# A token mixer in a new order: one rescaling of the input, 18 slabs by seven products, gates and retention in DRAM

## The chip, the core and the metric

One core of a Trainium2 chip runs the whole program in one launch. The metric is the device time in microseconds (us) of one execution. The engines are named as the profile names them: PE is TensorE's matmul, PEld its load of the stationary operand, DVE is VectorE, ACT is ScalarE, POOL is GpSimd, SP is SyncE, whose queue issues nearly all DMAs here. Each engine takes its instructions in the order in which they stand in its queue, and waits on semaphores for the others.

## What is computed

One encoder block over 512 positions of width 1024, in float32. The two feed-forward blocks are SwiGLU with 2816 hidden columns; the change leaves them alone, apart from shared helpers.

```python
x = x + 0.5 * swiglu_ffn(rms_norm(x, ffn1_norm), ffn1_w_gate, ffn1_w_up, ffn1_w_down)
h = rms_norm(x, mix_norm)
u_a, v_a, q_r, k_r, v_r, g_r, gate_a, gate_b = split(h @ w_in + b_in)      # eight times 1024 columns
a = spatial_gating(gelu(u_a), gelu(v_a), ...)        # layer norm of v, a 128x128 matrix per group and chunk
q, k = rotary(q_r), rotary(k_r) / 16                 # four heads of 256
r = bidirectional_retention(q, k, v_r, decay)        # scores x decay^|distance|, then x v
r = r * rsqrt(mean(r * r) + eps) * silu(g_r)         # per head
mix = sigmoid(gate_a) * (a @ w_branch_a) + sigmoid(gate_b) * (r @ w_branch_b)
x = x + mix @ w_out
x = x + 0.5 * swiglu_ffn(rms_norm(x, ffn2_norm), ...)
return rms_norm(x, final_norm)
```

## The kernel before

Activations lie with their columns on the partitions, eight tiles of 128 x 512 for the width of 1024. Every float32 product is made of three matmuls: each operand is split into a high part `hi` (rounded to the matmul's type) and a rest `lo`, and `mm3` (L96 to L99) adds hi x hi, hi x lo and lo x hi. So each weight slab of 1024 x 256 (1 MB) is loaded into `raw` (pool `wp`, two buffers), cast to `whi` by ACT (L91) and subtracted to `wlo` by DVE (L93), in the pool `wh` with three buffers of each. Activations are split likewise (`split`, L81 and L83). PSUM has eight banks.

A plain slab takes 2 x 8 x 3 = 48 matmuls over 512 columns. The feed-forward blocks also have the seven-product scheme of Strassen and Winograd for many of their slabs: `fast_weights` makes three sums of quarters of the weights (`s1`, `s2`, `s4`) and `Fast` runs seven products of half size, 7 x 4 x 3 = 84 matmuls over 256 columns, in four steps, with copies and additions of the partial results on ACT and DVE; it reads the input in four combined forms (`tforms`), which are made once per block.

The mixer (L577 to L833) uses plain slabs only. Its input `h2` is x times the norm's weight, not yet divided by the root mean square; that factor, `bc`, is multiplied into each projection as it leaves PSUM. For each of four heads come `rot` (q and k, with rotation by `cos` and `sin`), `pv_mm` of the head before (`pr`, with its norm `nr`), for even heads the v block `tok_block`, `scores` (times the decay table `E`), and `gate_r` (g, Silu), which also calls `r_out`. Then come the two halves of the gating unit's v (`pva`), the slabs of u with the chunk matrices (`psg`), and the merge: for each of four column groups the gates ga and gb (`pgt`), `pa` (a times `wa`) and `pb` (r times `wb`). r, a and the gates stay on the chip. A scheduler places the instructions of all engines in a fixed order when the program is built, from the order of the code, the data and the free buffers.

Of the kernel before, what the change touches and what calls it, by code (L numbers as in the profile page):

```python
# [40 lines left out]
def block_kernel(ctx, tc, xT, wg1, wu1, wd1, w_in, wa, wb, wo, wg2, wu2, wd2, cols_d, rows_d, ws_d, cos_d, sin_d, out, out_t):  # L41
# [152 lines left out]

    def ffn(tag, x, h, norm, wg, wu, wd, on_x, col, fp, p_fast, first=None, last=None, last_weights=None, aside=None):
# [16 lines left out]

        def make_tforms():

            left = [fp_n]

            def F(name):
                if left[0] > 0:
                    left[0] -= 1
                    return fp.tile([P, S], F32R, tag="f", name=name)  # L220
                return A(name)

            H = S // 2
            for k in range(KT // 2):
                ys = []
                for kk in (k, k + KT // 2):
                    y = T(f"{tag}y")
                    nc.scalar.activation(y, x[kk], AF.Copy, scale=cols[:, col + kk:col + kk + 1])
                    ys.append(y)
                y11, y12, y21, y22 = ys[0][:, 0:H], ys[0][:, H:S], ys[1][:, 0:H], ys[1][:, H:S]  # L230
                ta, tb = T(f"{tag}ta"), T(f"{tag}tb")
                t1, t2, t3, t4 = ta[:, 0:H], ta[:, H:S], tb[:, 0:H], tb[:, H:S]
                nc.vector.tensor_tensor(out=t1, in0=y12, in1=y11, op=ALU.subtract)
                nc.vector.tensor_tensor(out=t2, in0=y22, in1=t1, op=ALU.subtract)
                nc.vector.tensor_tensor(out=t3, in0=y22, in1=y12, op=ALU.subtract)
                nc.vector.tensor_tensor(out=t4, in0=y21, in1=t2, op=ALU.subtract)
                for i, t in ((1, ta), (3, tb)):
                    hi, lo = F(f"{tag}t_hi"), F(f"{tag}t_lo")
                    nc.scalar.copy(hi, t)
                    nc.vector.tensor_tensor(out=lo, in0=t, in1=hi.bitcast(F32), op=ALU.subtract)  # L240
                    tforms[i, k] = hi[:, 0:H], lo[:, 0:H]
                    tforms[i + 1, k] = hi[:, H:S], lo[:, H:S]

        def fast_weights(w, p):

            name = f"{tag}f"
            K2 = KT // 2
            raw = wp.tile([P, KT, 2 * P], F32, tag="raw", name=name + "_raw")
            nc.sync.dma_start(out=raw, in_=w[:, p * 256:(p + 1) * 256].rearrange("(k p) c -> p k c", p=P))
            x11, x12, x21, x22 = (raw[:, a * K2:(a + 1) * K2, i * P:(i + 1) * P] for i in range(2) for a in range(2))  # L250

            def V(t):
                return t.rearrange("p (k c) -> p k c", c=P)

            s1, s2, s4 = T(name + "_s1"), T(name + "_s2"), T(name + "_s4")
            nc.vector.tensor_tensor(out=V(s1), in0=x21, in1=x22, op=ALU.add)  # L256
            nc.vector.tensor_tensor(out=x21, in0=x11, in1=x21, op=ALU.subtract)
            hi = wh.tile([P, KT, 2 * P], F32R, tag="whi", name=name + "_whi")
            nc.scalar.copy(hi, raw)  # L259
            nc.vector.tensor_tensor(out=V(s2), in0=V(s1), in1=x11, op=ALU.subtract)  # L260
            nc.vector.tensor_tensor(out=V(s4), in0=x12, in1=V(s2), op=ALU.subtract)
            p1 = split(s1, name + "_s")
            lo = wh.tile([P, KT, 2 * P], F32R, tag="wlo", name=name + "_wlo")
            nc.vector.tensor_tensor(out=lo, in0=raw, in1=hi.bitcast(F32), op=ALU.subtract)  # L264
            p2 = split(s2, name + "_s")
            p4 = split(s4, name + "_s")
            f = {}
            for nm, a, i in (("X11", 0, 0), ("X12", 1, 0), ("S3", 0, 1), ("X22", 1, 1)):
                f[nm] = [tuple(t[:, a * K2 + k, i * P:(i + 1) * P] for t in (hi, lo)) for k in range(K2)]
            for nm, part in (("S1", p1), ("S2", p2), ("S4", p4)):  # L270
                f[nm] = [tuple(t[:, k * P:(k + 1) * P] for t in part) for k in range(K2)]
            return f

        class Fast:

            def __init__(self, f, t):
                self.f, self.t = f, t
                H = S // 2  # L280
                self.a, self.v, self.b = (PS(f"{tag}pf")[:, 0:H] for _ in range(3))
                self.c11, self.c12, self.c21, self.c22 = t[0][:, 0:H], t[0][:, H:S], t[1][:, 0:H], t[1][:, H:S]

            def prod(self, o, xf, yf, first):
                for k in range(KT // 2):
                    mm3(o, *self.f[xf][k], *yf(k), first and k == 0, k == KT // 2 - 1, not first)

            def run(self, step):
                H = S // 2

                def Y(a, j):
                    return lambda k: tuple(t[:, j * H:(j + 1) * H] for t in h[a * (KT // 2) + k])

                def Tf(i):
                    return lambda k: tforms[i, k]

                if step == 0:
                    self.prod(self.a, "X11", Y(0, 0), True)
                    self.prod(self.v, "S1", Tf(1), True)
                    nc.scalar.copy(self.c11, self.a)  # L300
                    nc.scalar.copy(self.c22, self.v)
                elif step == 1:
                    self.prod(self.a, "S2", Tf(2), False)
                    self.prod(self.b, "X12", Y(1, 0), True)
                    nc.scalar.copy(self.c12, self.a)
                    nc.vector.tensor_tensor(out=self.c11, in0=self.b, in1=self.c11, op=ALU.add)
                elif step == 2:
                    self.prod(self.a, "S3", Tf(3), False)
                    self.prod(self.v, "S4", Y(1, 1), False)
                    nc.vector.tensor_tensor(out=self.c22, in0=self.a, in1=self.c22, op=ALU.add)  # L310
                    nc.vector.tensor_tensor(out=self.c12, in0=self.v, in1=self.c12, op=ALU.add)
                else:
                    self.prod(self.a, "X22", Tf(4), False)

            def scaled(self):

                H = S // 2
                nc.vector.tensor_tensor(out=self.t[0], in0=self.t[0], in1=bc, op=ALU.mult)
                yield self.t[0]
                nc.vector.tensor_tensor(out=self.c21, in0=self.a, in1=bc[:, 0:H], op=ALU.mult)  # L320
                nc.vector.tensor_tensor(out=self.c22, in0=self.c22, in1=bc[:, H:S], op=ALU.mult)
                yield self.t[1]
# [724 lines left out]
```

## Time and profile before

| | us |
|---|---|
| three runs, median (lowest to highest) | 1251.41 (1251.28 to 1252.13) |
| the profiled execution, its own time | 1251.25 |
| its span, first to last instruction | 1249.2 |
| PE busy | 1240.2 |
| DVE busy | 827.1 |
| ACT busy | 500.7 |

Between the span and the time of the profiled execution lie 2.05 us. A matmul's busy time overlaps the next one's, so what a matmul costs is read from the distance of starts. A row of a timeline has the start, the duration, engine, line and operation, output and inputs by the program's names, and in brackets how long the engine was idle ahead of it and what ended that.

### The profile page before, as it was taken

The numbers are of one execution on the slowest core, as the hardware profiler recorded it, in microseconds if no ns is written. First come the engines' busy times: TensorE is split into PE (matmuls) and PEld (weight loads), VectorE is DVE, ScalarE is ACT, GpSimd is POOL, SyncE is SP. The second block draws the span as 40 slices with busy tenths as digits, with TensorE's granted clock in tenths as the row PEclk, the third lists the DMA queues.
The fourth block names the chain that finished last, engine by engine and source line by source line (L and its number), as shares of the span: only waits on it lengthen the run. The fifth ranks groups of instructions, "written<-read, shape, count | busy, mean of one in ns | idle before, by whom it ended". The sixth has DMA issues, their size and how long they took to land.

```text
span 1249.2 us, 15979 instructions
## 1 busy us (share of the span) xinstructions
PE 1240.2 (99%) x6714; PEld 1076.0 (86%) x6714; DVE 827.1 (66%) x1148; ACT 500.7 (40%) x643; POOL 7.6 (1%) x12
## 2 busy tenths in 40 slices
PE   9999999999999999999999999999999999999997
PEld 7889899989878888888888888888888989998997
DVE  6796679657777575675298334445587665976674
ACT  6553245424443342434344222223364423542352
POOL 0000000000000000000000000000000000000000
PEclk9999999999999999999999999999999999999999
DMA  8234323430463222233223333324232242334121
GB/s 264 75 101 136 101 68 102 135 102 26 127 222 99 75 69 93 68 101 135 68 68 101 101 101 102 101 93 149 96 98 92 82 135 68 102 102 135 60 93 68
DMA packets 115944, 128.47 MB, mean 103 GB/s; under 512 B 2977, under 2 KB 105377, under 8 KB 115873
## 3 DMA queue, kind: packets, MB, share of 16 engines
q1 hardware_dynamic: 115296, 126.63, 31.7%
q8 instruction: 52, 0.85, 0.3%
q10 hardware_dynamic: 576, 0.84, 0.2%
q14 instruction: 20, 0.16, 0.0%
HBM read 123.26 MB, written 4.19 MB: 102 GB/s over the span
## 4 chain that ended last, share of the span: by engine, by line
PE 92%; issue 6%; DVE 0%; POOL 0%; DMA 0%; ACT 0%; POOLq 0%; ACTq 0%
PE bpf L97 4%; PE bpf L99 4%; PE bpf L98 4%; PE apf L97 3%; PE apf L99 3%; PE apf L98 3%; PE bpd L97 3%; PE bpd L99 3%; PE bpd L98 3%; PE apd L97 2%; PE apd L98 2%; PE pgt L98 2%; PE pgt L97 2%; PE pgt L99 2%; PE apd L99 2%
## 5 line engine op out<-in xcount | busy, mean ns | idle before, releaser
L97 PE MATMUL apd<-ahid_hi,ad_whi 128*128 128x512 f32 x176 | 68.5, 389 | 0.0
L98 PE MATMUL apd<-ahid_lo,ad_whi 128*128 128x512 f32 x176 | 68.5, 389 | 0.0
L99 PE MATMUL apd<-ahid_hi,ad_wlo 128*128 128x512 f32 x176 | 68.5, 389 | 0.0
L97 PE MATMUL bpd<-bhid_hi,bd_whi 128*128 128x512 f32 x128 | 49.8, 389 | 0.0
L98 PE MATMUL bpd<-bhid_lo,bd_whi 128*128 128x512 f32 x128 | 49.8, 389 | 0.0
L99 PE MATMUL bpd<-bhid_hi,bd_wlo 128*128 128x512 f32 x128 | 49.8, 389 | 0.0
L81 ACT CAST bf_s_hi<-bf_s 128x512 fp32r<-128x512 f32 x42 | 25.7, 622 | 37.9 <-DVE bf_s L256 16.9
L81 ACT CAST af_s_hi<-af_s 128x512 fp32r<-128x512 f32 x42 | 25.8, 621 | 37.5 <-DVE af_s L256 16.1
L803 DVE TENSOR_TENSOR gt<-pgt,n_bc 128x512 f32<-128x512 f32 x16 | 11.1, 691 | 43.2 <-PE pgt L99 43.2
L99 PEld LDWEIGHTS apd<-ahid_hi,ad_wlo 128*128 128x128 f32 x176 | 33.0, 188 | 6.9
L97 PEld LDWEIGHTS apd<-ahid_hi,ad_whi 128*128 128x128 f32 x176 | 33.1, 188 | 6.8
L98 PEld LDWEIGHTS apd<-ahid_lo,ad_whi 128*128 128x128 f32 x176 | 33.1, 188 | 6.6
L259 ACT CAST af_whi<-af_raw 128x2048 fp32r<-128x2048 f32 x14 | 26.8, 1914 | 23.0 <-PE apd L98 17.5
L83 DVE TENSOR_TENSOR af_s_lo<-af_s,af_s_hi 128x512 fp32r<-128x512 f32 x42 | 28.7, 685 | 10.6 <-ACT af_s_hi L81 8.2
L83 DVE TENSOR_TENSOR bf_s_lo<-bf_s,bf_s_hi 128x512 fp32r<-128x512 f32 x42 | 28.6, 684 | 10.6 <-ACT bf_s_hi L81 8.2
L259 ACT CAST bf_whi<-bf_raw 128x2048 fp32r<-128x2048 f32 x14 | 26.8, 1913 | 21.5 <-PE bpd L98 17.3
L264 DVE TENSOR_TENSOR bf_wlo<-bf_raw,bf_whi 128x2048 fp32r<-128x2048 f32 x14 | 32.0, 2287 | 4.7 <-ACT bf_whi L259 4.6
L264 DVE TENSOR_TENSOR af_wlo<-af_raw,af_whi 128x2048 fp32r<-128x2048 f32 x14 | 32.0, 2287 | 3.5 <-ACT af_whi L259 3.5
L408 DVE SCALAR_TENSOR_TENSOR x<-apd,x 128x512 f32<-128x512 f32 x24 | 16.2, 685 | 24.1 <-PE apd L99 24.1
L99 PE MATMUL apf<-h_hi,af_wlo 128*128 128x256 f32 x112 | 31.7, 283 | 0.0
L97 PE MATMUL bpf<-bt_hi,bf_s_hi 128*128 128x256 f32 x112 | 31.7, 283 | 0.0
L99 PE MATMUL bpf<-h_hi,bf_wlo 128*128 128x256 f32 x112 | 31.7, 283 | 0.0
(470 smaller groups left out, 4176.8 us busy)
## 6 DMA issues: line engine op xcount, KB each, us to landing
af_raw<-in_wg SPq DMA_DIRECT2D x8, 1024.0 KB, 5.3
ad_raw<-in_wd SPq DMA_DIRECT2D x8, 1024.0 KB, 5.2
bf_raw<-in_wg SPq DMA_DIRECT2D x8, 1024.0 KB, 5.3
bd_raw<-in_wd SPq DMA_DIRECT2D x8, 1024.0 KB, 5.2
af_raw<-in_wu SPq DMA_DIRECT2D x6, 1024.0 KB, 5.3
bf_raw<-in_wu SPq DMA_DIRECT2D x6, 1024.0 KB, 5.4
bu_raw<-in_wu SPq DMA_DIRECT2D x5, 1024.0 KB, 5.4
au_raw<-in_wu SPq DMA_DIRECT2D x4, 1024.0 KB, 5.8
```

The lines of the kernel that those rows point to most:

```text
L81: nc.scalar.copy(hi, src)
L83: nc.vector.tensor_tensor(out=lo, in0=src, in1=hi.bitcast(F32), op=ALU.subtract)
L97: nc.tensor.matmul(o, lhi, rhi, start=first, stop=False, skip_group_check=more)
L98: nc.tensor.matmul(o, lhi, rlo, start=False, stop=False, skip_group_check=more)
L99: nc.tensor.matmul(o, llo, rhi, start=False, stop=last, skip_group_check=more)
L259: nc.scalar.copy(hi, raw)
L264: nc.vector.tensor_tensor(out=lo, in0=raw, in1=hi.bitcast(F32), op=ALU.subtract)
L408: nc.vector.scalar_tensor_tensor(out=x[m], in0=pd[j], scalar=0.5, in1=x[m], op0=ALU.mult, op1=ALU.add)
L803: nc.vector.tensor_tensor(out=t, in0=pg, in1=bc, op=ALU.mult)
```

## The change

The seven-product helpers (`t_forms`, `fast_weights`, `Fast`, `Plain`) are moved out of `ffn`, with the weights, the name and the inputs as arguments; their arithmetic is the same. In the mixer, 18 of the slabs of 256 columns now run by seven products: q and k of heads 2 and 3, g and ga of heads 1 to 3, all of u and gb. After the first q, k and v block, `rescale` multiplies x by the norm's weight and `bc` once, and all later projections read it (`hs`, and `tforms` made from it), so that their factor `bc` is dropped. Two slabs run as a pair, step by step in turn (`pair`): q with k, g with ga, u with gb. Gates ga and gb are thus made early; they and the retention's output r are written to DRAM (`g_dram`, `r_dram`) and read back in the merge, which runs all of `pb` first and then all of `pa`. The decay table `E` is made per head (`decay`) rather than for all four ahead.

```diff
@@ helpers, now outside of ffn @@
+    def t_forms(name, get, pool, left):
...
+    def fast_weights(w, c0, name):
+        raw = wp.tile([P, KT, 2 * P], F32, tag="raw", name=name + "_raw")
+        nc.sync.dma_start(out=raw, in_=w[:, c0:c0 + 256].rearrange("(k p) c -> p k c", p=P))
...
+        s1, s2, s4 = T(name + "_s1"), T(name + "_s2"), T(name + "_s4")
+        nc.vector.tensor_tensor(out=V(s1), in0=x21, in1=x22, op=ALU.add)
+        nc.vector.tensor_tensor(out=x21, in0=x11, in1=x21, op=ALU.subtract)
+        hi = wh.tile([P, KT, 2 * P], F32R, tag="whi", name=name + "_whi")
+        nc.scalar.copy(hi, raw)
+        nc.vector.tensor_tensor(out=V(s2), in0=V(s1), in1=x11, op=ALU.subtract)
+        nc.vector.tensor_tensor(out=V(s4), in0=x12, in1=V(s2), op=ALU.subtract)
+        p1 = split(s1, name + "_s")
+        lo = wh.tile([P, KT, 2 * P], F32R, tag="wlo", name=name + "_wlo")
+        nc.vector.tensor_tensor(out=lo, in0=raw, in1=hi.bitcast(F32), op=ALU.subtract)
+        p2 = split(s2, name + "_s")
+        p4 = split(s4, name + "_s")
...
+        def through(self, func, b1, b2):
+            nc.scalar.activation(self.t[0], self.t[0], func, bias=b1)
+            nc.scalar.activation(self.c21, self.a, func, bias=b2)
+            nc.scalar.activation(self.c22, self.c22, func, bias=b2)
+            return self.t
@@ the mixer @@
+    def pair(name, one, two, mid=None):
+        slabs = [Fast(w, name, hs, tforms) if isinstance(w, dict) else Plain(w, name, hs) for w in (one, two)]
+        for step in range(4):
+            for sl in slabs:
+                sl.run(step)
+            if step == 1 and mid is not None:
+                mid()
+        return slabs
+    def gate_out(slab, i, mp):
+        off = (OFF_GA, OFF_GB)[i] + 256 * mp
+        for j, t in enumerate(slab.through(AF.Sigmoid, bias(off), bias(off + P))):
+            nc.sync.dma_start(out=g_dram[i][256 * mp + P * j:256 * mp + P * (j + 1), :], in_=t)
+    def scores(hd, q, k):
+        E = decay(hd)
...
+    def r_out(hd, rt, slab):
+        col = OFF_G + 256 * hd
+        for d, g in enumerate(slab.through(AF.Silu, bias(col), bias(col + P))):
+            nc.vector.tensor_tensor(out=rt[d], in0=rt[d], in1=g, op=ALU.mult)
+            nc.sync.dma_start(out=r_dram[256 * hd + P * d:256 * hd + P * (d + 1), :], in_=rt[d])
+    def rescale():
+        for k in range(KT):
+            nc.vector.scalar_tensor_tensor(out=x[k], in0=x[k], scalar=cols[:, C_GM + k:C_GM + k + 1], in1=bc,
+                                           op0=ALU.mult, op1=ALU.mult)
+            hs.append(split(x[k], "hs"))
+    def g_pair(hd, st, wg_, wf, i, mp):
+        rt = []
+        slabs = pair("pg", wg_, wf, lambda: rt.extend(r_norm(st)))
+        return lambda: (r_out(hd, rt, slabs[0]), gate_out(slabs[1], i, mp))
...
+        for hd in range(1, HEADS):
+            qk = pair("qk", wq, wk)
+            if hd == 1:
+                tforms.update(t_forms("mt", lambda i: x[i], tp, tp_n))
+                del x
+            get = plain_w if hd == 1 else fast_w
+            wg_ = get(OFF_G + 256 * (hd - 1), "g")
+            q = rot(qk[0].plain(), OFF_Q, hd, "q")
+            st = pv_mm(hd - 1, v, pt)
+            k = rot(qk[1].plain(), OFF_K, hd, "k")
+            wf = get(OFF_GA + 256 * (hd - 1), "ga")
+            if hd == 2:
+                b_row = bvr_t(1)
+                pv = tok_block(hs, OFF_VR + 512, "pv")
...
+            end = g_pair(hd - 1, st, wg_, wf, 0, hd - 1)
+            if hd < HEADS - 1:
+                wq, wk = fast_w(OFF_Q + 256 * (hd + 1), "q"), fast_w(OFF_K + 256 * (hd + 1), "k")
+            end()
+            pt = scores(hd, q, k)
...
+    w1 = fast_w(OFF_G + 256 * 3, "g")
+    v_half(0, lambda: last_st.append(pv_mm(HEADS - 1, v, pt)))
+    w2 = fast_w(OFF_GA + 256 * 3, "ga")
+    end = g_pair(3, last_st.pop(), w1, w2, 0, 3)
+    w1 = fast_w(OFF_U, "u")
+    end()
+    v_half(1)
+    v_stats()
+    w2 = fast_w(OFF_GB, "gb")
+    for p in range(4):
+        slabs = pair("pu", w1, w2)
+        if p < 3:
+            w1, w2 = fast_w(OFF_U + 256 * (p + 1), "u"), fast_w(OFF_GB + 256 * (p + 1), "gb")
+        else:
+            tb = load_w(wb, 0, KT, 0, 256, "wb")
+        u_out(slabs[0], p)
+        gate_out(slabs[1], 1, p)
+        if p == 0:
+            v_norm(0)
+        elif p < 3:
+            s_pair(p - 1)
+    for i in range(KT):
+        t = T("rl")
+        nc.sync.dma_start(out=t, in_=r_dram[P * i:P * (i + 1), :])
+        r.append(split(t, "r"))
+    for mp in range(4):
+        gates = gate_in(1, mp)
+        for j in range(2):
+            pb = PS("pb")
+            proj(pb, tb, j, r)
+            nc.vector.tensor_tensor(out=gates[j], in0=pb, in1=gates[j], op=ALU.mult)
...
-        gates = []
-        for off, wt in ((OFF_GA, tga), (OFF_GB, tgb)):
-            for j in range(2):
-                pg = PS("pgt")
-                proj(pg, wt, j, h2)
-                t = T("gt")
-                nc.vector.tensor_tensor(out=t, in0=pg, in1=bc, op=ALU.mult)
-                nc.scalar.activation(t, t, AF.Sigmoid, bias=bias(off + P * (2 * mp + j)))
-                gates.append(t)
```

Where the order of the engines changes, first on DVE, around the v block of head 2. Before, from the first of its two low halves (`pv_wlo`) to the second:

```order
L93 TENSOR_TENSOR pv_wlo<-pv_raw,pv_whi 128x2048
L83 TENSOR_TENSOR r_lo<-rt,r_hi 128x512 x2
L646 TENSOR_TENSOR g<-pg,n_bc 128x512 x2
L608 TENSOR_TENSOR qt<-q,n_bc 128x512 x2
L615 SCALAR_TENSOR_TENSOR qc<-qt,cols,cos 128x512
L617 SCALAR_TENSOR_TENSOR qs<-qt,cols,sin 128x512
L615 SCALAR_TENSOR_TENSOR qc<-qt,cols,sin 128x512
L618 TENSOR_TENSOR qc<-qc,qs 128x512
L617 SCALAR_TENSOR_TENSOR qs<-qt,cols,cos 128x512
L93 TENSOR_TENSOR pv_wlo<-pv_raw,pv_whi 128x2048
```

The second one stands among the q rotation of head 2, before anything that reads `pr` of head 1. Now, from the k rotation and the norm's split to the first `pv_wlo`:

```order
L654 TENSOR_TENSOR kc<-kc,ks 128x512
L653 SCALAR_TENSOR_TENSOR ks<-qk_t,cols,cos 128x512
L238 TENSOR_TENSOR ga_s_4595<-ga_raw 128x512
L83 TENSOR_TENSOR k_lo<-kc,k_hi 128x512
L654 TENSOR_TENSOR kc<-kc,ks 128x512
L239 TENSOR_TENSOR ga_raw<-ga_raw 128x4x128
L242 TENSOR_TENSOR ga_s_4596<-ga_s_4595,ga_raw 128x512
L83 TENSOR_TENSOR k_lo<-kc,k_hi 128x512
L243 TENSOR_TENSOR ga_s_4597<-ga_raw,ga_s_4596 128x512
L246 TENSOR_TENSOR ga_wlo<-ga_raw,ga_whi 128x2048
L83 TENSOR_TENSOR ga_s_lo<-ga_s_4595,ga_s_hi 128x512
L93 TENSOR_TENSOR pv_wlo<-pv_raw,pv_whi 128x2048
```

The low half has moved behind the k rotation, the three sums of the `ga` weights and `ga_wlo`; the norm's sum `nr_sq` (L119) stands four rows ahead of the first row shown.

Second, on ACT, around the weights of the gating unit's second v half (`pva_whi`). Before, from the root of the norm of head 2 on (`g` is the Silu gate):

```order
L177 ACT_TABLE_LOAD
L177 ACTIVATE nr_y<-nr_pbc,eps 128x512
L91 CAST pva_whi<-pva_raw 128x2048
L81 CAST r_hi<-rt 128x512 x2
L647 ACT_TABLE_LOAD
L647 ACTIVATE g<-g,cols 128x512 x2
L91 CAST pva_whi<-pva_raw 128x2048
L723 ACT_TABLE_LOAD
L723 ACTIVATE va<-va 128x512 x3
L91 CAST u_whi<-u_raw 128x2048
```

Each `pva_whi` stands with one table load between it and the next. Now, from the first Silu of the last g and ga pair (L313 and L315 are Silu or Sigmoid on sums, L314 on PSUM):

```order
L315 ACT_TABLE_LOAD
L315 ACTIVATE pg_t<-pg_t,cols 128x256
L241 CAST u_whi<-u_raw 128x2048
L81 CAST u_s_hi<-u_s_6098 128x512
L314 ACT_TABLE_LOAD
L314 ACTIVATE pg_t<-pg,cols 128x256
L81 CAST u_s_hi<-u_s_6099 128x512
L313 ACT_TABLE_LOAD
L313 ACTIVATE pg_t<-pg_t,cols 128x512
L81 CAST u_s_hi<-u_s_6100 128x512
L314 ACTIVATE pg_t<-pg,cols 128x256
L91 CAST pva_whi<-pva_raw 128x2048 x2
```

Both casts of `pva` have moved behind all Silu and Sigmoid activations of that pair, their table loads and the casts of the `u` weights.

## Rows read from the trace of the kernel before

**Rows 1.** The page, part 1: busy time, share of the span, instructions.

```profile
PE 1240.2 (99%) x6714; PEld 1076.0 (86%) x6714; DVE 827.1 (66%) x1148; ACT 500.7 (40%) x643; POOL 7.6 (1%) x12
```

**Rows 2.** Busy time by stretch; columns: us, engines, PEclk, DMA share, GB/s.

```profile
180.00:345.00 165.00, 165.00 (x1075) 151.60 (x1074) 125.13 (x193) 71.53 (x100) 0.88 (x1) 1.00 0.32 100
355.00:877.00 522.00, 520.90 (x2327) 430.21 (x2326) 309.12 (x381) 180.47 (x190) 4.02 (x2) 1.00 0.31 100
```

**Rows 3.** PE by time, `g` and `q` slabs; columns: start, us, engine, line, operation.

```profile
450.60 0.39 PE L97 MATMUL pg<-h_hi,g_whi 128*128 128x512 f32 x1
...
472.36 0.39 PE L98 MATMUL q<-h_lo,q_whi 128*128 128x512 f32 x1
```

**Rows 4.** PE by time, in a seven-product pair of the first feed-forward block.

```profile
229.81 0.29 PE L97 MATMUL apf<-at_hi,af_whi 128*128 128x256 f32 x1
...
236.64 0.28 PE L97 MATMUL apf<-at_hi,af_whi 128*128 128x256 f32 x1
```

**Rows 5.** PE waits; columns: waiter, waited for, us in total, times, longest.

```profile
PE n_pbc L162 <- DVE n_diag_hi L152: 0.6, 1, 0.6
```

**Rows 6.** ACT groups of one shape; columns: busy us, mean ns, idle before.

```profile
L177 ACT ACT_TABLE_LOAD x6 | 7.7, 1283 | 6.7 <-PE n_pbc L175 4.3 <-PE nr_pbc L175 2.4
...
L804 ACT ACTIVATE gt<-gt,cols 128x512 f32<-128x512 f32 x16 | 11.5, 720 | 23.8 <-DVE gt L803 23.8
...
L91 ACT CAST pv_whi<-pv_raw 128x2048 fp32r<-128x2048 f32 x4 | 7.6, 1910 | 13.9 <-PE n_pbc L163 5.9 <-PE pg L98 4.5 <-PE q L98 3.5
...
L81 ACT CAST k_hi<-kc 128x512 fp32r<-128x512 f32 x8 | 5.0, 622 | 9.2 <-DVE kc L618 9.2
...
L887 ACT ACTIVATE n_xg<-xb,cols 128x256 f32<-128x256 f32 x8 | 4.0, 495 | 0.0
...
L305 ACT COPY atg<-apf 128x256 f32<-128x256 f32 x8 | 3.0, 372 | 2.2 <-PE apf L99 2.2
```

**Rows 7.** DVE by time, around the k rotation of head 2.

```profile
476.87 2.29 DVE L93 TENSOR_TENSOR pv_wlo<-pv_raw,pv_whi 128x2048 fp32r<-128x2048 f32 x1
...
484.50 0.74 DVE L615 SCALAR_TENSOR_TENSOR kc<-kt,cols,cos 128x512 f32<-128x512 f32 x1
...
486.49 0.69 DVE L618 TENSOR_TENSOR kc<-kc,ks 128x512 f32<-128x512 f32 x1
487.09 0.74 DVE L617 SCALAR_TENSOR_TENSOR ks<-kt,cols,cos 128x512 f32<-128x512 f32 x1
487.75 2.28 DVE L93 TENSOR_TENSOR g_wlo<-g_raw,g_whi 128x2048 fp32r<-128x2048 f32 x1
489.95 0.68 DVE L83 TENSOR_TENSOR k_lo<-kc,k_hi 128x512 fp32r<-128x512 f32 x1
```

**Rows 8.** PE by time, where the second v block of head 2 begins.

```profile
489.13 0.39 PE L97 MATMUL pv<-pv_whi,h_hi 128*128 128x512 f32 x1
489.36 0.39 PE L98 MATMUL pv<-pv_wlo,h_hi 128*128 128x512 f32 x1
```

**Rows 9.** ACT by time, there.

```profile
489.39 0.60 ACT L117 ACTIVATE nr_sq<-pr 128x512 f32<-128x512 f32 x1 [1.57 <-PE pr L99]
```

**Rows 10.** ACT by time, a table load between two activations of head 1.

```profile
522.47 1.28 ACT L177 ACT_TABLE_LOAD   x1 [2.35 <-PE nr_pbc L175]
523.77 0.69 ACT L177 ACTIVATE nr_y<-nr_pbc,eps 128x512 f32<-128x512 f32 x1
```

**Rows 11.** PE by time, first and last matmuls of the span.

```profile
1.19 4.32 PE L463 MATMUL warm<-warm 128*128 128x512 bf16 x10 [1.19 <-DVE warm L63]
...
1242.55 0.28 PE L99 MATMUL bpl<-last_hi,bhid_lo 128*128 128x256 f32 x1
```

**Rows 12.** Busy time and granted clock by stretch, end of the span.

```profile
1243.00:1247.60 4.60, 0.00 (x0) 0.00 (x0) 1.46 (x5) 1.23 (x3) 0.67 (x1) 1.00 0.28 103
1247.80:1249.20 1.40, 0.00 (x0) 0.00 (x0) 0.00 (x0) 0.00 (x0) 0.00 (x0) 0.50 0.00 0
```

**Rows 13.** DMA issues of one kind: KB each, us to landing.

```profile
xb<-x_dram SPq DMA_DIRECT2D x8, 256.0 KB, 6.0
```

More of the change, by code (lines that the diff above doesn't have):

```diff
@@ L204, in weights @@
                 return wgt, load_w(wu, 0, KT, p * 256, 256, f"{tag}u{p}")
+        p_both = (4, 5, 7, 8, 9, 10)
         tforms = {}
-        p_both = (4, 5, 7, 8, 9, 10)
         def make_tforms():
[L215 to L322, printed above, removed]
@@ L551, in block_kernel @@
     ffn("a", x, h, norm, wg1, wu1, wd1, on_x1, C_G1, fp, 3, first, aside=tables)
[L552 removed]
+    del h
     def bias(col):
         return cols[:, C_B + col // P:C_B + col // P + 1]
[L558 to L566 removed]
+    r_dram = dram.tile([D, S], F32, name="r_dram")
@@ new lines, in rot_first @@
+    def rot_first(off, name, wt, between=None):
+        nonlocal bc
+        tt = []
+        for j in range(2):
+            pq = PS(name)
+            proj(pq, wt, j, h2)
+            tt.append(pq)
+            if j == 0 and between is not None:
+                between()
+        if bc is None:
+            bc = norm2.spread_sb()
+        for j in range(2):
+            t = T(name + "t")
+            nc.vector.tensor_tensor(out=t, in0=tt[j], in1=bc, op=ALU.mult)
+            tt[j] = t
+        return rot(tt, off, 0, name)
@@ new lines, in block_kernel, with v_half @@
+    stats = gp.tile([P, NT, 2, nc.vector.BN_STATS_DIM], F32, name="stats")
+    def v_half(half, between=None):
+        bv = row("bv", R_BV, half)
+        pv = tok_block(hs, OFF_V + 512 * half, "pva", between)
+        for j in range(NT):
+            t = A("va", F32)
+            nc.vector.tensor_tensor(out=t, in0=pv[j], in1=bv, op=ALU.add)
+            nc.scalar.activation(t, t, AF.Gelu)
+            nc.vector.bn_stats(out=stats[:, j, half, :], in_=t)
+            vv[j][half] = t
+    mv = gp.tile([P, NT, 2], F32, name="mv")
@@ new lines, in block_kernel, with u_out, s_pair @@
+    us = {}
+    def u_out(slab, p):
+        off = OFF_U + 256 * p
+        for j, t in enumerate(slab.plain()):
+            u = A("ut", F32)
+            nc.scalar.activation(u, t, AF.Gelu, bias=bias(off + P * j))
+            us[2 * p + j] = u
+    def s_pair(p):
+        for j in range(2):
+            i = 2 * p + j
+            g_ = i // 2
+            po = PS("psg")
+            for n in range(NT):
+                nc.tensor.matmul(po[:, n * CHUNK:(n + 1) * CHUNK],
+                                 vv[n][i // 4][:, (i % 4) * P:(i % 4 + 1) * P], ws[:, g_, :],
+                                 start=True, stop=True)
+            t = T("st")
+            nc.vector.tensor_tensor(
+                out=t.rearrange("p (n c) -> p n c", c=CHUNK),
+                in0=po.rearrange("p (n c) -> p n c", c=CHUNK),
+                in1=bs[:, g_ * CHUNK:(g_ + 1) * CHUNK].unsqueeze(1).broadcast_to([P, NT, CHUNK]),
+                op=ALU.add)
+            nc.vector.tensor_tensor(out=t, in0=t, in1=us.pop(i), op=ALU.mult)
+            a.append(split(t, "a"))
```

505 lines of the change are left out of this document (260 added, 245 removed).

## The prediction

> **The bound.** I began with the busy times: TensorE (PE) is busy 1240.2 of 1249.2 us, VectorE (DVE) 66%, ScalarE (ACT) 40% [rows 1]. By stretches, the token mixer (355 to 877 us) has PE busy 520.90 of 522.00 us and DVE 309.12 [rows 2]; PE's longest wait behind its first instruction is 0.6 us [rows 5]. So the sum of the matmuls sets the time, and everything else is hidden as long as it is ready in time. The change therefore has two questions: how much matmul time goes, and whether PE still never waits. The profiled execution took 1251.25 us (span 1249.2), against a median of 1251.41 us; the sum starts from 1251.25.
>
> **The gain.** A plain slab of 256 columns is 2 x 8 x 3 = 48 matmuls over 512 columns. Two starts that lie 96 matmuls apart are at 450.60 and 472.36, so one takes 21.76 / 96 = 0.2267 us [rows 3], and a slab 10.88 us. A seven-product slab is 7 x 4 x 3 = 84 matmuls over 256 columns. Two starts 57 apart are at 229.81 and 236.64, so one takes 0.1198 us [rows 4], and a slab 10.06 us. The gain is 0.82 us a slab and 14.7 us for 18 (four of q and k, three each of g and ga, four each of u and gb). No other matmul is added or dropped.
>
> **The cost.** A fast slab has seven half-size sums and splits of 0.69 us, a low half of 2.29 us and up to five combinations of 256 columns on DVE; the scaling by 1/rms that each projection had is dropped. This costs nothing while it is off PE's path. In the first feed-forward block such slabs already run, at 125.13 us of DVE in 165.00 us of PE without one idle moment [rows 2], so the arithmetic alone is no harm there.
>
> The one-time work is beside matmuls too: `rescale` is 16 DVE operations, 11 us, beside the 96 matmuls of the first v block, 21.8 us; `t_forms` is 16 half and 8 whole ones, some 12 us, beside plain slabs, in a mixer in which DVE had 309 of 522 us [rows 2]; a head's decay adds two DVE operations, an Exp and a table load. If that cover were gone, PE would wait for at most those 23 us once; I see no place where it is. The 24 stores of gates and r (256 KB each) stand on SP's queue, where a store waits for its Sigmoid or product and the weight loads behind it wait too; those loads are for slabs two ahead, so I count nothing, but see place E.
>
> What matters is the order: each engine takes its instructions in turn, and the new mixer often puts the preparation of PE's next weights behind something that waits for PE's last result. I followed five such places along the order, each step by its row. The steps: 0.26 us from the next possible matmul (489.13) to the ACT instruction that had waited for the product before it (489.39) [rows 8, 9]; Square 0.60 [rows 9]; on DVE back to back three rotation steps in 1.99 (484.50 to 486.49), a 512-column operation 0.60 (486.49 to 487.09), a low half 2.20 (487.75 to 489.95) or 2.29 until it is done [rows 7]; on ACT a weight cast 1.91, a table load 1.28, an activation with bias 0.72 or 0.49 for half the columns, a cast 0.62, a copy 0.37 [rows 6].
>
> *Place A, v of head 2.* Before, `pv_wlo` was made at 476.87 and first read at 489.36 [rows 7, 8]: ten us early. Now DVE meets first the sum `nr_sq` (L119), which waits for the Square of the last `pr` product, and has three rotation steps, nine other operations, `ga_wlo` and one more split before `pv_wlo` (first tables of the order). From the end of `pr`: 0.26 + 0.60 + 0.60 + 1.99 + 9 x 0.60 + 2.20 + 0.60 + 2.29 = 13.9 us. PE has four matmuls of `pv` and three of `pg` to run without it, 1.3 us. PE idles 12.7 us.
>
> *Place B, g and ga of head 2 (loop turn 3).* The same queue up to `ga_wlo`: 0.26 + 0.60 + 0.60 + 1.99 + 9 x 0.60 + 2.29 = 11.1 us; PE has 34 half-size matmuls, 4.1 us. 7.1 us.
>
> *Place C, first v half of the gating unit.* `pva_wlo` lies behind the last score tile: 0.26, eight operations, `g_wlo` 2.20, one split, 2.29, together 10.2 us; PE has six matmuls, 1.4 us. 8.8 us.
>
> *Place D, second v half.* Here ACT is late (second tables): behind the product `nr_pbc` come five table loads (6.4), the root (0.7), six activations (3.4), `u_whi` (1.9), three casts (1.9), then `pva_whi` (1.9) and on DVE `pva_wlo` (2.3); with 0.26 that is 18.7 us. PE has 72 half-size and five whole matmuls in between, 9.7 us. 9.0 us. The loads stand singly between Silu and Sigmoid, since the two gates of a pair are finished in turn.
>
> *Place E, the first `pb`.* r now comes back from DRAM as `rl` and is split there. Behind the last u and gb products ACT has a copy (0.37), `wb_whi` (1.91), table load and Gelu (2.0), table load and Sigmoid (1.77), `r_hi` of the first tile (0.62) and a second `wb_whi` (1.91); DVE then has `wb_wlo` (2.29) ahead of `r_lo` of the second tile (0.69). With 0.26 this is 11.8 us; PE has twelve half-size and thirteen whole matmuls, 4.4 us. 7.4 us.
>
> These are 45.0 us; in three or four other places the same arithmetic gives 0.3 to 1 us each, together 2.5. Bounds: with each queue's own work alone, never waiting for the other engine in between, the five come to 40; with whole durations (0.69 for 0.60 and so on) to 50. I take 47.5 with the small ones, because before's rows show DVE operations following each other at 0.60. Loads and stores: a 256 KB tile is read back in 6.0 us [rows 13]; gates are asked for a pass ahead, so I count nothing, but if `rl` comes a whole read later than its cast could run, place E grows by up to 6.
>
> **The clock.** The first ten matmuls of the span, behind idleness, took 4.32 us [rows 11], 0.43 each: the lower level, 1.2 GHz. Behind the last matmul (1242.55) the granted clock stands at 1.00 until 1247.6 and at 0.50 from 1247.8 [rows 11, 12]. Stalls of 7 to 13 us are longer than that idleness, so some of them should end at the lower level. Ten matmuls at 0.43 instead of 0.2267 cost 2.05 us, for five places 10.2; a few matmuls run inside each stall, and what is late behind it hides a part, so I take half, 5 us, of bounds 0 and 10.2. The Trainium skill, "TensorE: Matmul & The Clock Gate", section "HAM oscillation — how this bites in real kernels", has the same mechanism, a wait in each turn of a loop that sends PE back to the lower clock every time; by it all five places pay, and the sum would be 1294. This kernel's trace shows only the one fall at its end.
>
> **Sum.** 1251.25 - 14.7 + 47.5 + 5 = 1289 us, slower by 3%.
>
> **Table loads.** In the trace a load starts at 522.47 and its activation at 523.77: 1.30 us, with nothing behind it [rows 10]. The Trainium skill, "ScalarE: Activation LUTs", section "What ACT_TABLE_LOAD costs", adds to the 1283 ns of the load a drain of about 1380 ns. By that page place D would be longer by 5 x 1.38 = 6.9 us and E by 2.8, an estimate of 1299 us; the trace doesn't agree.
>
> **The rivals.**
> 1. *The covers hold: faster.* The preparation would still be ready, as in the feed-forward blocks [rows 2], and only the matmul gain is left: 1251.25 - 14.7 = 1236.6 us. It would need each of the five chains to be hidden, at the least that the stalls together stay below the 14.7 us gained, some 2.9 us a place: that decides. At A this means `pv_wlo` within 4.2 us of the end of `pr`, of which Square and two low halves alone take 5.3. Only other weights in the place of those in the order would do it. 8%.
> 2. *The stalls are there, but smaller, so that the sum lies within 0.2% of before or between it and 1262*: the chains would have to be a third of the above. 3% for no change, 5% for 1254 to 1262.
> 3. *The clock falls at all five places*: 1251.25 - 14.7 + 47.5 + 10.2 = 1294 us. 14%.
> 4. *DVE becomes the bound in the u and gb loop.* A pass has two fast slabs, 2 x (2.29 + 7 x 0.69 + 5 x 0.42) = 18.4 us of DVE, in 20.1 us of PE (168 half-size matmuls); `v_norm` adds 12 operations (8.2) in the first pass, two `s_pair` some 5.5 each. The four passes want 73.6 + 8.2 + 11 = 93 of 80.5 us, of which preparation made ahead hides some; if nothing hides it, 12 us more, 1301. The half-size duration of 0.42 is an estimate from 0.69 by the ratio of ACT's rows for whole and half [rows 6]. 8%.
> 5. *A table load costs twice its row*: the seven of places D and E would take 7 x 1.28 = 9.0 us more [rows 6], 1298 us; the 1.30 us of [rows 10] speaks against it. 4%.
> My forecast, stalls of 40 to 53 us with none to most of the clock's cost, has the remaining 58%.
>
> **The numbers.** The likeliest case is 1289. Its own ends: 1251.25 - 14.7 + 40 = 1276.5, and 1251.25 - 14.7 + 53 + 10.2 = 1300. To hold 8 in 10 the range takes in rivals 3 to 5 for the most part and a part of the smaller stalls: 1268 to 1303. A difference of 0.2%, 2.5 us, is about what a measurement of this kernel can tell from none. Faster by more: rival 1, 0.08. Same: 0.03. Slower: 0.89.
>
> **The proof.** Right: in the mixer of the changed kernel, PE waits, which were next to nothing, add up to some 45 us, in five clusters: ahead of `pv` for `pv_whi`/`pv_wlo` (12 to 13 us), `pg` for `ga_wlo` (7), twice `pva` for `pva_whi`/`pva_wlo` (9 each), and `pb` for `r_hi`/`r_lo` (7); PE's start-to-start times stay at 0.2267 and 0.1198 outside of them; the granted clock dips behind some. Wrong: few and short PE waits and a span near 1235 (rival 1); one long row of small waits in the u and gb loop (rival 4); half-rate matmuls behind every cluster (rival 3); gaps behind each table load (rival 5); waits for `rl` by DMA (the DRAM bound of place E).

## The result and the profile after

The changed kernel takes 1289.6 us (median of four runs, 1288.54 to 1289.87) against 1251.49 us before: 1.0301 times the time, 95% interval 1.0288 to 1.0315. The forecast was 1289, with a range of 1268 to 1303. The profiled execution has a span of 1287.7 us, 38.5 more than before.

The page of the changed kernel, its first part, the clock in 40 slices and the chain that ended last:

```profile
PE 1238.9 (96%) x7362; PEld 1104.7 (86%) x7362; DVE 913.5 (71%) x1324; ACT 585.8 (45%) x805; POOL 7.6 (1%) x12
...
PEclk9999999999999997998899998999999999999999
...
PE 91%; DVE 4%; ACT 3%; issue 1%; DMA 0%; POOL 0%; POOLq 0%; ACTq 0%
```

The same clock row and chain of the kernel before:

```profile
PEclk9999999999999999999999999999999999999999
...
PE 92%; issue 6%; DVE 0%; POOL 0%; DMA 0%; ACT 0%; POOLq 0%; ACTq 0%
```

PE is busy for about as long as before ([rows 1]: 1240.2), in a longer span. The sevens and eights in the middle of the clock's row are new, and the chain now has 4% of DVE and 3% of ACT, where it had none.

PE's waits in the changed kernel (waiter, waited for, us in total, times, longest), where [rows 5] had 0.6 us as the longest behind the start:

```profile
PE pva L97 <- ACT pva_whi L91: 15.1, 2, 7.6
PE pv L97 <- ACT pv_whi L91: 11.3, 1, 11.3
PE pg L97 <- ACT ga_whi L241: 7.2, 1, 7.2
PE pb L97 <- ACT r_hi L81: 5.2, 1, 5.2
...
PE pu L99 <- DVE gb_wlo L246: 0.8, 1, 0.8
PE pv L98 <- DVE pv_wlo L93: 0.7, 1, 0.7
```

These are the five places that the prediction named: `pv` (A), `pg` (B), `pva` twice (C and D) and `pb` (E), each waiting for a cast that ACT makes late. Next, stretches of the changed kernel: for places A to E in turn the idle time and the time behind it, and last the whole mixer (us, then busy PE, PEld, DVE, ACT, POOL, then the granted clock, DMA share and GB/s):

```profile
484.90:496.60 11.70, 0.44 (x2) 0.02 (x1) 10.38 (x15) 6.65 (x8) 0.00 (x0) 0.70 0.00 0
496.60:503.20 6.60, 6.45 (x16) 5.00 (x17) 4.01 (x5) 1.04 (x2) 0.00 (x0) 0.50 0.83 249
578.00:585.60 7.60, 0.44 (x4) 0.24 (x2) 7.50 (x13) 3.71 (x5) 0.00 (x0) 0.74 0.00 0
585.60:590.00 4.40, 4.32 (x19) 4.28 (x20) 4.10 (x4) 2.13 (x6) 0.00 (x0) 0.50 0.24 43
611.20:619.40 8.20, 0.77 (x4) 0.30 (x2) 7.97 (x12) 6.12 (x7) 0.00 (x0) 0.78 0.59 139
619.40:622.80 3.40, 3.39 (x8) 2.37 (x9) 3.36 (x3) 0.47 (x1) 0.00 (x0) 0.52 0.78 219
668.00:676.70 8.70, 1.12 (x10) 0.91 (x8) 6.72 (x9) 8.64 (x10) 0.00 (x0) 0.84 0.36 83
676.70:681.00 4.30, 4.20 (x10) 3.07 (x11) 2.29 (x1) 1.66 (x2) 0.00 (x0) 0.54 1.00 342
785.20:791.10 5.90, 0.81 (x7) 0.61 (x6) 2.29 (x1) 5.84 (x7) 0.00 (x0) 0.90 0.47 145
791.10:797.30 6.20, 6.13 (x15) 4.51 (x16) 5.05 (x6) 5.48 (x9) 0.00 (x0) 0.55 0.83 279
355.00:916.00 561.00, 520.17 (x2976) 459.18 (x2975) 397.75 (x558) 266.51 (x353) 4.03 (x2) 0.96 0.36 114
```

In each idle stretch the granted clock falls (its mean is 0.70 to 0.90 there), and behind it PE is busy at 0.50 to 0.55, the lower level. While PE idles, one engine has hardly a pause: DVE at A (10.38 of 11.70 us), B (7.50 of 7.60) and C (7.97 of 8.20), ACT at D (8.64 of 8.70) and E (5.84 of 5.90). The averages of the page, 71% and 45%, don't show that. Over the mixer PE is busy for 520.17 us of 561, where [rows 2] had 520.90 of 522; what the seven products save is filled up by matmuls at half rate.

Place A, step by step. ACT, the Square that begins the chain and the cast that PE waits for (start, duration):

```profile
485.43 0.60 ACT L117 ACTIVATE nr_sq<-pr 128x512 f32<-128x512 f32 x1 [2.00 <-issue]
...
494.71 1.89 ACT L91 CAST pv_whi<-pv_raw 128x2048 fp32r<-128x2048 f32 x1
```

DVE there, from the norm's sum to the low half:

```profile
486.06 0.69 DVE L119 TENSOR_TENSOR nr_sq<-nr_sq 128x512 f32<-128x512 f32 x1 [1.73 <-ACT nr_sq L117]
...
494.31 2.29 DVE L246 TENSOR_TENSOR ga_wlo<-ga_raw,ga_whi 128x2048 fp32r<-128x2048 f32 x1 [0.16 <-ACT ga_whi L241]
496.52 0.68 DVE L83 TENSOR_TENSOR ga_s_lo<-ga_s,ga_s_hi 128x512 fp32r<-128x512 f32 x1
497.12 2.29 DVE L93 TENSOR_TENSOR pv_wlo<-pv_raw,pv_whi 128x2048 fp32r<-128x2048 f32 x1
```

PE there:

```profile
496.65 2.07 PE L97 MATMUL pv<-pv_whi,hs_hi 128*128 128x512 f32 x4 [11.31 <-ACT pv_whi L91]
498.52 0.41 PE L97 MATMUL pg<-hs_hi,g_whi 128*128 128x256 f32 x1
...
499.46 0.80 PE L98 MATMUL pv<-pv_wlo,hs_hi 128*128 128x512 f32 x1
```

PE could have gone on at 485.17; the Square starts 0.26 later, DVE meets `nr_sq` at 486.06, and `pv_wlo` begins at 497.12 and is done at 499.41. That is 14.2 us behind `pr`; the prediction's sum was 13.9. PE starts at 496.65 with `pv_whi`, and its first `pv_wlo` matmul stands at 499.46.

Place D, on ACT, the beginning and the end of its chain:

```profile
660.58 1.28 ACT L177 ACT_TABLE_LOAD   x1 [1.58 <-PE nr_pbc L175]
661.88 0.69 ACT L177 ACTIVATE nr_y<-nr_pbc,eps 128x512 f32<-128x512 f32 x1
662.58 1.28 ACT L315 ACT_TABLE_LOAD   x1
...
674.83 1.88 ACT L91 CAST pva_whi<-pva_raw 128x2048 fp32r<-128x2048 f32 x1
```

From 660.32 (the start of the first load less 0.26) to the end of `pva_wlo`, 679.04, it is 18.7 us, as summed. A load takes 1.28 us, and the activation before it and the one behind it follow at once: 661.88 + 0.69 = 662.57 is where the second load starts. The Trainium skill's drain of 1.38 us at each switch ("ScalarE: Activation LUTs", section "What ACT_TABLE_LOAD costs") is not in this trace.

Place E, on ACT:

```profile
784.88 1.90 ACT L91 CAST wb_whi<-wb_raw 128x2048 fp32r<-128x2048 f32 x1
786.80 1.28 ACT L830 ACT_TABLE_LOAD   x1
...
788.84 1.28 ACT L314 ACT_TABLE_LOAD   x1
...
790.50 0.61 ACT L81 CAST r_hi<-rl 128x512 fp32r<-128x512 f32 x1
791.01 1.90 ACT L91 CAST wb_whi<-wb_raw 128x2048 fp32r<-128x2048 f32 x1
792.81 3.22 ACT L81 CAST r_hi<-rl 128x512 fp32r<-128x512 f32 x6
```

Cast of `wb`, table load, Gelu, table load, Sigmoid and only then `r_hi` at 790.50, which PE had needed at 785.85; the second `wb_whi` stands between the first `r_hi` and the others. On DVE the splits of the second tile and those behind it follow:

```profile
795.15 3.09 DVE L83 TENSOR_TENSOR r_lo<-rl,r_hi 128x512 fp32r<-128x512 f32 x5
```

The second tile's `r_lo` is the first of these five and, at 0.69 us, done at 795.84. That is 11.5 us behind the start of the chain (784.35, the last copy's start less 0.26); the prediction's sum was 11.8.

### The profile page after: what moved, and what is told of

Its sections match the earlier page's. It is cut to its first block, busy times and chain, and to the rows that moved or that the text cites. A ratio compares the mean times of both kernels' runs of the same rounds, so it can differ in the third digit from the quotient of the medians.

```text
span 1287.7 us, 17789 instructions
## 1 busy us (share of the span) xinstructions
PE 1238.9 (96%) x7362; PEld 1104.7 (86%) x7362; DVE 913.5 (71%) x1324; ACT 585.8 (45%) x805; POOL 7.6 (1%) x12
## 4 chain that ended last, share of the span: by engine, by line
PE 91%; DVE 4%; ACT 3%; issue 1%; DMA 0%; POOL 0%; POOLq 0%; ACTq 0%
PE bpf L97 4%; PE apf L97 4%; PE apf L99 4%; PE bpf L99 4%; PE bpf L98 4%; PE apf L98 4%; PE apd L97 3%; PE apd L98 3%; PE apd L99 3%; PE bpd L97 3%; PE bpd L99 3%; PE bpd L98 3%; PE pg L97 2%; PE pg L99 2%; PE qk L97 2%; PE pg L98 2%
## 5 line engine op out<-in xcount | busy, mean ns | idle before, releaser
L97 PE MATMUL pva<-pva_whi,hs_hi 128*128 128x512 f32 x64 | 26.2, 428 | 15.1 <-ACT pva_whi L91 15.1
L83 DVE TENSOR_TENSOR af_s_lo<-af_s,af_s_hi 128x512 fp32r<-128x512 f32 x42 | 28.8, 685 | 10.6 <-ACT af_s_hi L81 8.2
```

What stands on the lines that cost most here:

```text
L83: nc.vector.tensor_tensor(out=lo, in0=src, in1=hi.bitcast(F32), op=ALU.subtract)
L97: nc.tensor.matmul(o, lhi, rhi, start=first, stop=False, skip_group_check=more)
```

## The experiments

Two theories were to be told apart: that PE waits because of the *place* of its next weights in the queues of ACT and DVE, and that these engines simply have too much work in the mixer. Then there were the price of the clock, that of the table loads, and the part of the DRAM. "Excess" below is the distance from one PE start to the next, less 0.2267 or 0.1198 us, summed over a place. In the changed kernel it is 14.9 us at A, 10.3 at B, 9.3 at C, 9.9 at D and 8.2 at E, together 52.6 (the expectations below have 52.4). Of these, 39.6 are the idle times and 13.0 lie behind them, in matmuls at the lower clock. Beside the first four runs the kernel before took 1251.63 us, beside the others 1251.36; "less" is against the 1289.6 us of the changed kernel.

### One move at A

```diff
+            if hd == 2:
+                pvw = load_w(w_in, 0, 4, OFF_VR + 512, 512, "pv0")
             q = rot(qk[0].plain(), OFF_Q, hd, "q")
             st = pv_mm(hd - 1, v, pt)
             k = rot(qk[1].plain(), OFF_K, hd, "k")
-            wf = get(OFF_GA + 256 * (hd - 1), "ga")
+            if hd != 2:
+                wf = get(OFF_GA + 256 * (hd - 1), "ga")
             if hd == 2:
...
-                pv = tok_block(hs, OFF_VR + 512, "pv")
+                pv = tok_block(hs, OFF_VR + 512, "pv", w0=pvw)
...
+                wf = get(OFF_GA + 256 * (hd - 1), "ga")
```

> The changed kernel with one move: the first weights of the second v block (pv0) are loaded and split ahead of the q rotation and of the norm of pr, and the ga weights of that turn behind them; no work is added or dropped. Theory (place in the queue): the PE wait for pv_whi of 11.3 us and the half-rate matmuls behind it, together 14.9 us in the trace, and the late pv1 (1.2 us) go, the other four places stay: 1289.6 - 15 to 16 = 1274 us. Rival (DVE and ACT have too much work in the mixer, wherever it stands): the same work is late elsewhere, 1287 to 1290 us.

Measured: 1273.75 us (1273.41 to 1275.7), 1.0182 of before (1.0165 to 1.0199): 15.9 us less. PE's waits for `pv` are gone from the list, and the other four stand in it as they did: `pva` 15.1 us, `pg` 7.2, `pb` 5.2. The excess at B to E is 10.3, 9.3, 9.9 and 8.1 us. The work is the same, so it was its place.

### One move at C

```diff
-    w1 = fast_w(OFF_G + 256 * 3, "g")
-    v_half(0, lambda: last_st.append(pv_mm(HEADS - 1, v, pt)))
+    w1 = []
+    v_half(0, lambda: (w1.append(fast_w(OFF_G + 256 * 3, "g")), last_st.append(pv_mm(HEADS - 1, v, pt))))
+    w1 = w1.pop()
```

> The changed kernel with one move: the weights of the last g slab are asked for behind the first half of the first gating v block rather than ahead of it; no work is added or dropped. Theory (place in the queue): the 9.4 us that the trace has ahead of and behind pva_whi (7.6 idle, the rest at half rate) go: 1280 us. Rival (too much work): the g weights come late for their pair instead, 1287 to 1290 us.

Measured: 1279.85 us (1279.32 to 1280.52), 1.0226 (1.021 to 1.0241): 9.8 us less, against an excess of 9.3 there. Of the two waits for `pva_whi` PE's list keeps one, of 7.7 us (D), and it has none for the `g` weights that were asked for later.

### The new order with plain slabs

```diff
     def fast_w(off, name):
-        return fast_weights(w_in, off, name)
+        return plain_w(off, name)
...
             if hd == 1:
-                tforms.update(t_forms("mt", lambda i: x[i], tp, tp_n))
                 del x
```

`plain_w`, which the changed kernel uses for its first slabs, loads and splits the same 256 columns as they are; the activation then reads the outputs straight from PSUM, without the adds ahead of it.

> The changed kernel with plain slabs in place of all 18 seven-product slabs, and without their combined input forms; order of the code, rescaling, DRAM for gates and r unchanged. Theory (the stalls at A to D come from the sums and low halves of the seven-product weights that stand between a late result and the next weights; E comes from r in DRAM): the matmul time goes back up by 14.7 us, places A to D are empty, E (8.2 us in the trace) stays: 1251.5 + 7 to 8 = 1259 us. Rival (the new order stalls by itself): 1289.6 + 14.7 = 1304 us. Rival (DRAM and order cost nothing): 1251 us.

Measured: 1256.98 us (1256.54 to 1257.72), 1.0043 (1.0028 to 1.0058). PE's longest wait there, and its mixer as one stretch:

```profile
PE pb L97 <- ACT r_hi L81: 5.4, 1, 5.4
```

```profile
355.00:880.00 525.00, 519.59 (x2317) 430.20 (x2316) 292.21 (x352) 209.81 (x218) 4.03 (x2) 0.99 0.38 120
```

Places A to D are empty and E stays, with an excess of 7.8 us; the mixer's start loses 2.3 us less than before, so the time is 5.4 us above it. So the order by itself, with one rescaling and with gates and r in DRAM, costs only place E. A to D come from what the seven-product weights add on DVE and ACT (sums, splits, low halves, and the adds of the outputs), part of which stands between PE's last result and its next weights: with all five moves (below) the two have 395.61 and 265.68 us in the mixer, against 292.21 and 209.81 here, which is 5.7 and 3.1 us more for each of the 18 slabs, the combined input forms included.

### All five moves

A and C as above; at B the `ga` weights of head 2 are asked for ahead of the q rotation; at D the second v block's first weights ahead of the end of the last gate pair and the u weights behind the block's first half; at E three of the eight r tiles are read and split ahead of the last u and gb pair:

```diff
             wg_ = get(OFF_G + 256 * (hd - 1), "g")
+            if hd == 3:
+                wf = get(OFF_GA + 256 * (hd - 1), "ga")
...
-    w1 = fast_w(OFF_U, "u")
+    vw = load_w(w_in, 0, 4, OFF_V + 512, 512, "pva0")
     end()
-    v_half(1)
+    w1 = []
+    v_half(1, lambda: w1.append(fast_w(OFF_U, "u")), vw)
+    del vw
+    w1 = w1.pop()
...
     for p in range(4):
+        if p == 3:
+            for i in range(3):
+                r_in(i)
         slabs = pair("pu", w1, w2)
...
-    for i in range(KT):
+    for i in range(3, KT):
+        r_in(i)
```

> The changed kernel with all five moves: pv0 ahead of the rotation (A), the ga weights of head 2 ahead of the q rotation (B), the last g weights behind the first half of the v block (C), the second v block's weights ahead of the end of the last gate pair and the u weights behind its first half (D), three of the eight r tiles read back and split ahead of the last u and gb pair (E). Same arithmetic. Theory (place in the queue): of the 52.4 us lost at the five places some 50 go, B keeps about 2: 1239 us, 1% faster than before. Rival (too much work for DVE and ACT): a part comes back in the u and gb loop and elsewhere, 1250 to 1289 us. Rival (the half-size matmuls don't give 14.7 us in the mixer): the stalls go but the time stays near 1251.

Measured: 1238.26 us (1238.06 to 1238.65), 0.9894 of before (0.9879 to 0.9908). PE's waits there down to 0.4 us, and the mixer as one stretch:

```profile
PE pg L97 <- ACT pg_t L281: 1.6, 1, 1.6
...
PE pu L99 <- DVE gb_wlo L246: 1.0, 1, 1.0
PE qk L97 <- ACT k_whi L241: 0.4, 1, 0.4
```

```profile
355.00:865.00 510.00, 507.01 (x2978) 450.66 (x2977) 395.61 (x558) 265.68 (x353) 4.03 (x2) 1.00 0.39 125
```

DVE has 395.61 us of work in the mixer, the changed kernel 397.75: the same, now in 510 us rather than 561, and PE's clock stays at the upper level (1.00). The theory of too much work is out. What was moved at A is seen in two rows of DVE:

```profile
480.25 2.29 DVE L93 TENSOR_TENSOR pv_wlo<-pv_raw,pv_whi 128x2048 fp32r<-128x2048 f32 x1 [1.77 <-ACT pv_whi L91]
...
488.46 0.68 DVE L119 TENSOR_TENSOR nr_sq<-nr_sq 128x512 f32<-128x512 f32 x1
```

`pv_wlo` now stands ahead of the norm's sum `nr_sq`, not behind it. Against the plain order this is 18.7 us less. From PE's first start in the mixer to its last it is 17.97 us (540.82 and 522.85), of which 3.25 are the smaller excess; that leaves 14.72 for the matmuls, where 14.7 were summed. Outside the stalls they kept the distances of 0.2267 and 0.1198 us, from which the excess is counted. The rest of the 18.7 lies outside the mixer, most of it behind PE's last matmul.

### The gaps filled with matmuls

```diff
+    def fill(n):
+        pw = PS("fill")
+        for _ in range(n):
+            nc.tensor.matmul(pw, hs[0][0][:, 0:P], hs[0][0], start=True, stop=True)
...
+                fill(48)
                 pv = tok_block(hs, OFF_VR + 512, "pv")
```

That is place A; likewise 30 stand at B, 32 at C, 32 at D and 21 at E.

> The changed kernel with matmuls that nobody reads put into the five gaps, in PE's order right ahead of the waits: 48 at A, 30 at B, 32 at C, 32 at D, 21 at E, each 0.2267 us, so 10.9, 6.8, 7.3, 7.3 and 4.8 us, a little under the idle times of the trace (11.5, 7.4, 7.6, 7.8, 5.3). PE then hardly idles and its clock should stay at the upper level. In the trace 12.9 us of the 52.4 at the five places lie behind the idle time, with matmuls at half rate. Theory (the half rate costs only about half of it, since the low halves wlo and the r splits are late anyway and come in the meantime): 1289.6 - 5 = 1284 us, 1281 to 1286, and short waits for wlo appear. Rival (the clock costs all of it): 1277 us. Rival (the clock costs nothing): 1289 us.

Measured: 1281.97 us (1280.78 to 1284.06), 1.0247 (1.0231 to 1.0262). With 163 matmuls more, 37 us of them, the kernel is 7.6 us faster. Two of its stretches (A and E), then PE behind the filling at A:

```profile
480.00:520.00 40.00, 37.37 (x176) 30.64 (x175) 23.02 (x29) 13.98 (x17) 0.00 (x0) 1.00 0.26 80
...
778.00:800.00 22.00, 21.05 (x100) 16.93 (x99) 12.77 (x15) 13.14 (x16) 0.00 (x0) 1.00 0.63 203
```

```profile
497.42 1.21 PE L97 MATMUL pv<-pv_whi,hs_hi 128*128 128x512 f32 x4 [0.46 <-ACT pv_whi L91]
...
500.39 0.40 PE L98 MATMUL pv<-pv_wlo,hs_hi 128*128 128x512 f32 x1
```

The granted clock is 1.00 in all five, so the half rate is gone. But the scheduler also ordered PE's other matmuls anew. Between these two rows 16 half-size `pg` matmuls are done, where the changed kernel has three, so that `pv_wlo` is no longer waited for. Ahead of the first low half B has 19 matmuls for 10, C 14 for 6 and D 17 for 5. At the five places the excess, the filling counted with it, falls from 52.6 to 41.5 us, by 11.1. In the changed kernel 5.8 us of it stand behind the first matmul that a late low half or split sets (worked out below), and only that much can be the clock's price while the order stays; the other 5.3 would then be lateness that other matmuls now cover. Elsewhere the kernel loses again: 2.7 us at the second half of the v block, where it was 1.2, and 0.7 ahead of the mixer. So the run shows that filled gaps keep the clock up, but not the price of the clock alone. The expected waits for `wlo` didn't come at A to D; at E there is one of 0.6 us for `r_lo`.

### Three table loads less

```diff
-        for d, g in enumerate(slab.through(AF.Silu, bias(col), bias(col + P))):
+        for d, g in enumerate(slab.through(AF.Sigmoid if hd == 3 else AF.Silu, bias(col), bias(col + P))):
```

> The changed kernel with Sigmoid in place of Silu for the gate g of head 3 alone (this changes that part of the computation), which takes three of the five table loads out of place D; two casts of the u sums also move behind pva_whi (1.2 us of ACT). Theory (a load costs its row, 1.28 us): ACT reaches pva_whi 3.8 + 1.2 = 5.0 us earlier, the idle time there falls from 7.8 to about 3 and the half rate behind it goes, less a wait for pva_wlo: 1284 to 1285 us. Rival (a load costs 2.66 us): the place is all but empty, 1280 us. Rival (the loads run while ACT would wait anyway): 1288 to 1290 us.

Measured: 1284.07 us (1282.87 to 1284.17), 1.0259 (1.0241 to 1.0276): 5.5 us less. ACT at place D, the first load and the cast that PE waits for:

```profile
660.98 1.28 ACT L177 ACT_TABLE_LOAD   x1 [1.58 <-PE nr_pbc L175]
...
670.79 1.90 ACT L91 CAST pva_whi<-pva_raw 128x2048 fp32r<-128x2048 f32 x1
```

From the load to the cast it is 9.8 us, where it was 14.25: 4.4 less, for three loads at 1.28 (3.8) and two casts moved behind (1.2), less an idle moment of 0.7 ahead of `u_whi`. A price of 2.66 us a load would have given 8.0 for the loads alone. The half rate did not go, as the expectation had it: the idle time that is left, 3.3 us, ends at the lower clock too (0.55 from 672.7 to 676.0), and the excess at D is 4.8 us, for 9.9.

### One move at E

The lines for r as above, without the other moves.

> The changed kernel with one move: three of the eight r tiles are read back from DRAM and split ahead of the last u and gb pair. Theory (at E PE waits for r's splits behind ACT's queue, not for DRAM): the 8.2 us at E go, the u and gb loop loses at most 1: 1281 to 1283 us. Rival (the reading back is what is late): the pair ahead waits for its operands or E keeps most, 1287 to 1290 us.

Measured: 1282.1 us (median of three runs, 1281.56 to 1283.14), 1.0247 (1.023 to 1.0264): 7.5 us less. The profiled execution, a fourth, took 5470.64 us, with its matmuls of 512 columns 0.69 to 1.45 us apart in place of 0.2267; it is left out, and its trace is not read. Reading r back from DRAM is early enough; it was the place of its splits. The moves one by one give 15.9 + 9.8 + 7.5 = 33.2 us at A, C and E, which leaves 18.1 of the 51.3 for B and D, where the excess was 20.2 and 1.8 remains at B. B and D were moved only together with the others.

### A step apart in the g and ga pairs

```diff
-        for step in range(4):
-            for sl in slabs:
-                sl.run(step)
-            if step == 1 and mid is not None:
...
+        for step in range(5):
+            if step < 4:
+                slabs[0].run(step)
+            if step > 0:
+                slabs[1].run(step - 1)
+            if step == 1:
                 mid()
```

(for the pairs with `mid`, on top of the five moves)

> The kernel with all five moves, and in the g and ga pairs the ga slab runs one step behind the g slab, so that its weights have 2.9 us more. Theory (what is left at B is the late ga weights and the copy behind them): the 1.8 us that the five moves left there fall to about 0.5: 1235 to 1237 us, against 1238.3. Rival (the step's offset only moves the wait, or the last ga products end alone and late): 1238 to 1240 us.

Measured: 1235.43 us (1235.18 to 1235.87), 0.9873 of before (0.9859 to 0.9888), the fastest here: 1.3% less than before, 4.2% less than the changed kernel. PE's longest wait there, behind the start:

```profile
PE pu L99 <- DVE gb_wlo L246: 0.7, 1, 0.7
```

## Why the prediction was right

**The gain.** 14.7 us were summed; the five moves against the plain order show 14.7 in the mixer. Without the stalls the kernel reaches 1235 to 1238 us, where rival 1 had put it, at 1236.6. The rival's price was right and its condition wasn't met: the weights were not ready.

**The five places.** The sum went by when the low half, or the split, is there, and that can be checked place by place. PE's first matmul that reads it came late by 13.0 us at A (499.46, against 485.17 + 1.27), 8.6 at B, 9.1 at C and 9.1 at D. At E the second tile's `r_lo` was there 7.0 us late (795.84, against 785.85 + 13 x 0.2267); PE, still at the lower clock, came to it at 796.97. Together these are 46.8 us; the prediction had 12.7, 7.1, 8.8, 9.0 and 7.4, together 45.0. B was too short: `nr_sq` stood behind `q_lo`, which waits for casts that ACT makes behind the Exp and its table load, and that was not in the sum.

**The clock.** All five idle times ended at the lower level, as rival 3 had it, though E's was only 5.3 us. Rival 3's price of 10.2 us was not paid. 13.0 us lie behind the idle times, but 46.8 - 39.6 = 7.2 of them pass while the low halves and splits are late anyway, which leaves 52.6 - 46.8 = 5.8 us. The prediction took 5, half of ten matmuls a place, because what is late anyway hides a part: the mechanism was right, and the term 0.8 us too small. This is worked out from the changed kernel's trace; no run has the upper clock with PE's order unchanged. It is also not the same each time: at C, with the same idle time of 7.6 us, the excess is 9.3 us in the changed kernel and 10.6 in the run with three table loads less. The Trainium skill ("TensorE: Matmul & The Clock Gate", section "HAM oscillation — how this bites in real kernels") tells of a loop whose matmuls start at the lower clock after each wait for a transfer; this trace agrees, with 0.50 to 0.55 behind the waits shown, though here the waits are for casts.

**The small places** were put at 2.5 us; `pv1`, `k_whi`, `gb_wlo` and the start of the first q and k pair show 1.2, 0.7, 1.0 and 0.55, together 3.5. The mixer's start lost 2.3 us less than before (0.7 for 3.0), which the prediction didn't have. So -14.7 + 46.8 + 5.8 + 3.5 - 2.3 = 39.1 us, for 38.5 measured between the spans. The hit within 1 us is in part luck: the places, the clock and the small places were 1.8, 0.8 and 1.0 us too low, and the 2.3 us at the start took most of that back.

**The other rivals.** DVE didn't become the bound in the u and gb loop: single waits of 0.8 us. DRAM cost nothing by itself, as the plain order and the move at E show. Table loads cost their row.

## What to carry to other kernels

When a change saves work on the engine that sets the time, follow the queues of the others from each late result to the next operand, with durations that the trace already has; five such sums, with the matmuls' gain and a price for the clock, gave this time within 1%, and said which lines to move. Prepare the next weights ahead of whatever waits for the result of the current ones, and put the preparation that isn't urgent behind it; the same work then cost 51 us less. Of a stall of several microseconds on TensorE, count matmuls at half rate behind it too.

## What the runs showed of the hardware

The granted clock fell in all five idle stretches of PE, the shortest of 5.3 us, and the matmuls behind them took 0.43 us for 512 columns and 0.21 for 256, until 3.3 to 6.7 us later. With matmuls that nobody reads in the gaps it stayed at 1.00, and the kernel was 7.6 us faster; since PE's other matmuls were ordered anew with it, the clock's share of that stays open. Without the gaps it was 51.3 us faster. A table load took its 1.28 us, and the activations around it followed at once.
